# Norm sums by a row of ones and scales broadcast through DRAM, in a decoder layer of parallel mixers

## The chip, the cores and the metric

The kernel runs on one core of one Trainium2 chip. The metric is the device time of one execution in microseconds, as the median of several runs. A core has five engines with a queue each: TensorE (PE, matrix products; its weight loads are listed as PEld), VectorE (DVE), ScalarE (ACT), GpSimd (POOL) and SyncE (SP, which here issues most DMAs). Each engine takes its instructions in the order in which the program has them, and waits at an instruction until what it needs is there.

## The reference, cut to what matters

One layer on 1040 tokens (16 meta tokens and 1024 others) of 1024 channels. The places that the change touches are the sums of squares over channels, the pool map and their surroundings:

```python
h = rms_norm(h_res, pre_norm_g[i])
z = h @ w_in[i]                      # 1024 x 7328
(pv, pg, cq, ckv, kr, mg, cu, cg, sbcx, sg, gl) = split_cols(z)
# pool branch: four windows, then a 64 x 64 map per group
p = stack([(cs - lag) / cnt - g ...]); y = einsum('blgc,gcd->blgd', p, pool_w) * pool_scale
# latent attention
q  = rms_norm(c_q, q_norm_g) @ w_uq        # 256 channels, 8 heads of 64 + 32
kv = rms_norm(c_kv, kv_norm_g) @ w_ukv     # 128 channels
# conformer branch, after its depthwise convolution of width 31
z = silu(layer_norm(z, ln_g, ln_b))        # 256 channels
# short convolution of width 3, then gates, output projections, sum
m = sum(sigmoid(g_i) * y_i); x = x + rms_norm(m @ w_o, post_norm_g)
```

## The kernel before

**Three stages.** First the projection `z = h @ w_in`: channels on partitions, tokens on the free axis, 128 + 128 output channels times two halves of the tokens at a time, by seven half-size products instead of eight (a Strassen-like scheme). A product is split in three rounded passes: a number is held as a rounded high part and the rest (type float32r), and high x high, high x low and low x high are added up. The seven products of a pair of column blocks go to the PSUM banks `ps_pa`, `ps_pb`, `ps_pc` and `ps_pd`, 84 passes of 512 columns a pair, or two units of 84 passes of 256 or 272 columns where the meta tokens are among them. Then attention by heads (`ps_s` scores, `ps_o` outputs), with the output projections of three branches (`ps_y<-bo,whl`) put between. Then attention's own output projection and the last product with `w_o`.

**Side tasks.** Everything else of the first stage stands in four lanes of tasks (`task_conv`, `task_kv`, `task_q`, `task_norm`, `task_short`, `task_pool`, `task_w`, `task_so`, `task_first`). After each product of the projection `pump` advances each lane by its pace (0.9, 0.9, 1.1 and 0.5 steps). The list `pairs` sets the order of the column blocks; a task begins once the columns that it needs are written. The tasks' data lie in DRAM between steps (`z_dram` and others), and their tiles come from small rings of buffers (`t4`, `t2`, `w1`).

**What sets the order.** All instructions are first recorded, then a planner (`Plan.flush`) sorts them by a priority and by its own durations for engines and transfers, and issues each engine's instructions in that order. The engines then take them as they stand. Each instruction is issued at one line, so that views of the profile show L362 for nearly all, and one reads by tiles.

**Norm sums before** (`rs_row`, lines 943 to 969). The squares `sq` lie with channels on partitions. For 128 tokens at a time they are the stationary operand of a full-precision product with a column `ones`, so that a column of 128 sums comes out (`ps_x<-ones,sqk` and the like, four columns in a set). DVE divides and adds epsilon, POOL raises to the power -0.5 (`rs`). Four transposes of the columns, each widened to 128, put the scale of each token on all partitions (`ps_x<-ident,rs`), and DVE multiplies with it out of PSUM. `task_kv` does so for 512, 512 and 16 tokens, `task_q` twice, `task_norm` twice. `task_norm` also has a mean: a full-precision product of 512 columns with ones (`ps_y<-lsq,ones`). `task_pool` has four full-precision products of 512 columns with its map (`ps_y<-pd,pw`).

**Attention's start.** `load_q`, `load_kv` and the loads of masks, ones and zeros (lines 1438 to 1457) are issued on SP as the first stage's buffers come free. For head 0 the maxima of the scores are found in the first stage (`task_first`, once per half of the tokens) and come through `top_dram`.

Of the kernel before, what the change touches and what calls it, by code (L numbers as in the profile page):

```python
# [68 lines left out]
CH_KV = [(0, 512), (512, 512), (1024, 16)]  # L69
# [402 lines left out]
def trunk_kernel(ctx, tc, a):  # L472
# [34 lines left out]
    DVE.memset(ones, 1.0)  # L507
    mhalf = const.tile([P, 16], F32, name="mhalf")
# [29 lines left out]
    ones_dram = dram.tile([4, L], F32, name="ones4")  # L538
    top_dram = dram.tile([4, 2, 4, P], F32, name="top")
# [403 lines left out]
    def rs_row(sqs, of, scale=None, tag="x", ns=0):  # L943

        n = sqs[0].shape[1]
        p = min(n, P)
        if len(sqs) > 1:  # L950
            add(POOL, sqs[0], sqs[0], sqs[1])
        sq = sqs[0]
# [5 lines left out]
        rs = col([P, 4], "rs")[:p, :n // p]  # L958
        with plan.late(ns):
            DVE.tensor_scalar(rs, pc, 1.0 / of, EPS, op0=ALU.mult, op1=ALU.add)  # L960
            POOL.tensor_tensor(rs, rs, mhalf[:p, :n // p], op=ALU.pow)
        if scale:
            DVE.tensor_scalar(rs, rs, scale, None, op0=ALU.mult)
        yield
        out = bank(tag)[:, :n]
        for j in range(n // p):
            PE.transpose(out[:, p * j:p * (j + 1)], rs[:, j:j + 1].to_broadcast([p, P]), ident[:p, :p])
        yield
        return out
# [77 lines left out]
    def task_norm(c):  # L1047
# [5 lines left out]
        sq = [t2([P, 512], name="lsq")]  # L1053
        add(POOL, sq[0], acc[0], acc[1])
        pa = bank("y")
        PE.matmul(pa, ones.to_broadcast([P, P]), sq[0], start=True, stop=True)
        yield
        sq.append(t2([P, 512], name="lsq"))
# [4 lines left out]
        rs = yield from rs_row(sq, 256, tag="y")  # L1063
        for m in range(2):
            g, b, hb = (t_[:, r + m:r + m + 1] for t_, r in ((par, R_LG), (par, R_LB), (par, R_HLB)))
            DVE.scalar_tensor_tensor(acc[m], acc[m], g, rs, op0=ALU.mult, op1=ALU.mult)
            th, cg = t2([P, 512], name="lth"), t2([P, 512], name="cgt")
            ACT.activation(th, acc[m], AF.Tanh, scale=0.5, bias=hb)
            ld(cg, z_dram[f"cg{m}"][:, s_])
# [3 lines left out]
            mul(POOL, cg, acc[m], cg)  # L1073
            store_bo(2 + m, c, cg)
            yield

    def task_short(m, c):
# [5 lines left out]
        ld(xx, z_dram[f"x{m}"][:, p0:p0 + 514])  # L1083
        mul(POOL, u, u, xx)
        yield
        v = t2([P, 512], name="v")
# [7 lines left out]
        b, g = t2([P, 512], name="bt"), t2([P, 512], name="gt")  # L1094
        ld(b, z_dram[f"b{m}"][:, s_])
        ld(g, z_dram[f"sg{m}"][:, s_])
# [5 lines left out]

    def task_pool(m, c):

        s_ = slice(512 * c, 512 * (c + 1))
        pw = tp.tile([P, P], F32, tag="wraw", bufs=2, name="pw")
        POOL.memset(pw, 0.0)
        for g in range(2):
            ld(pw[64 * g:64 * g + 64, 64 * g:64 * g + 64], a["pool_w"][0, 2 * m + g])
        n = 512 + 15  # L1110
        pv_, sa, sb = (t2([P, n], name=i) for i in ("pv", "sa", "sb"))
        pd = t2([P, 512], name="pd")
        p0 = NM - 15 + 512 * c
        ld(pv_, z_dram[f"pv{m}"][:, p0:p0 + n])
        yield
# [10 lines left out]
        yield  # L1126
        pa = bank("y")
        g = t2([P, 512], name="pgt")
        ld(g, z_dram[f"pg{m}"][:, s_])
        PE.matmul(pa, pw, pd, start=True, stop=True)  # L1130
# [17 lines left out]
    def task_q(c):  # L1148
# [3 lines left out]
        cq, sq = t4([P, 2, 512], name="cq"), t4([P, 2, 512], name="sqq")  # L1152
        for m in range(2):
            ld(cq[:, m], z_dram[f"cq{m}"][:, s_])
            ACT.activation(sq[:, m], cq[:, m], AF.Square)
        yield
        rs = yield from rs_row([sq[:, 0], sq[:, 1]], 256, QK ** -0.5)
# [65 lines left out]
    def task_first(c):  # L1223

        n = NM + 512 * (c + 1)
        for h in range(FIRST):
            k_ = t4([QK, L], F32R, name="k0")[:, :n]
            k_rows(k_, h, lambda x: x[:, 0, :n])
            q_ = t4([QK, 512], F32R, name="q0")
            ld(q_, q_dram[c][h][:, 0])  # L1230
# [3 lines left out]
            mx = tp.tile([P, 4, 3], F32, name="mx")  # L1234
            POOL.memset(mx, NEG)
            yield from row_maxima(c, mx, q_, k_, mask, bank)
            mr = tp.tile([P, 4], F32, name="mr")
            DVE.tensor_reduce(mr, mx, axis=AX.X, op=ALU.max)
            pm = bank()
            PE.transpose(pm[:4, :P], mr, ident)  # L1240
            DVE.tensor_copy(mask[:4].bitcast(F32R), pm[:4, :P])
            for r in range(4):
                ld(top_dram[r:r + 1, c, r], mask[r:r + 1])

    def task_kv():
# [25 lines left out]
        ckv, sq = t4([P, L], name="ckv"), t4([P, L], name="sqk")  # L1271
        ld(ckv, z_dram["ckv"])
        ACT.activation(sq, ckv, AF.Square)
        yield
        for n0, n in CH_KV:
            rs = yield from rs_row([sq[:, n0:n0 + n]], P, ns=1500)
            DVE.scalar_tensor_tensor(ckv[:, n0:n0 + n], ckv[:, n0:n0 + n], par[:, R_KVG:R_KVG + 1], rs,
# [666 lines left out]
```

## Time and profile before

| | before |
|---|---|
| runs | 967.77, 968.78, 968.97 us, median 968.78 |
| span of the profiled execution, first to last instruction | 967.1 us (its time as a run is not given apart) |
| granted PE clock, mean | 0.998 |
| first scores of attention | 639.4 us |
| DMA | 203.03 MB, mean 210 GB/s |

How to read the lines that follow in the prediction. The busy table gives busy time, share of the span and count of instructions of each engine. A stretch row gives a stretch in us, its length, then busy us (and count) of PE, PEld, DVE, ACT and POOL, the granted clock, the DMA engines' busy share and GB/s. A row of the order of time gives start, length, engine, line, operation, out<-in, shape and a count; neighbours of one kind are merged, and what stands in brackets is the idle time before it and what ended it. A row of the groups ends with busy us and mean ns of one, then the idle time before. Matmuls overlap, so that a row's length runs into the next row's start.

### The profile page before, as it was taken

How to read it: one execution, taken by the hardware profiler on the slowest of the kernel's cores; microseconds unless marked ns; L12 is line 12 of the kernel's file. 1: busy time of each engine (PE TensorE's matmuls, PEld its weight loads, DVE VectorE, ACT ScalarE, POOL GpSimd, SP SyncE). 2: the span in 40 equal slices, each digit the busy share in tenths (PEclk: the TensorE clock that was granted, in tenths of full speed). 3: DMA queues.
4: the chain of work that ended last, by engine and by line, in shares of the span. 5: the costliest groups of instructions: out<-in, count | busy, mean ns of one | idle time of the engine just before them, and what ended most of it. 6: DMA issues, size and time to landing. Idle time of an engine off the chain costs nothing.

```text
span 967.1 us, 15246 instructions
## 1 busy us (share of the span) xinstructions
PE 952.0 (98%) x5003; PEld 809.9 (84%) x5003; DVE 692.5 (72%) x1111; ACT 449.4 (46%) x914; POOL 680.3 (70%) x630
## 2 busy tenths in 40 slices
PE   8999999999999999999999999999999999999996
PEld 7999899889888887888788878888888878788885
DVE  5856959988879855554446767436878888799857
ACT  7743233444443455554434344356555565324622
POOL 5957555666577887896679679656567786747955
PEclk9999999999999999999999999999999999999999
DMA  7144556758787687787655687699899663773543
GB/s 258 32 126 144 170 190 213 234 195 257 230 261 260 206 250 207 212 264 216 211 161 160 204 267 274 222 316 264 266 227 289 194 196 116 261 255 109 187 148 142
DMA packets 136329, 203.03 MB, mean 210 GB/s; under 512 B 19671, under 2 KB 83158, under 8 KB 135482
## 3 DMA queue, kind: packets, MB, share of 16 engines
q1 hardware_dynamic: 127274, 185.28, 62.2%
q10 hardware_dynamic: 8656, 15.74, 4.4%
q0 software_dynamic: 320, 1.05, 0.3%
q8 instruction: 39, 0.64, 0.3%
q14 instruction: 40, 0.33, 0.1%
HBM read 129.11 MB, written 72.88 MB: 209 GB/s over the span
## 4 chain that ended last, share of the span: by engine, by line
PE 88%; POOL 4%; DVE 3%; issue 2%; ACT 1%; DMA 1%; SPq 0%; DVEq 0%; ACTq 0%; POOLq 0%
PE ps_pa L362 16%; PE ps_pb L362 16%; PE ps_pc L362 15%; PE ps_o L362 9%; PE ps_u L362 7%; PE ps_s L362 7%; PE ps_pd L362 7%; PE ps_y L362 6%; PE ps_x L362 5%; POOL S L362 1%; DMA x<-in_x_dram 1%; POOL lsq L362 1%; DVE th L362 1%; POOL pt L362 0%; ACT junk L362 0%
## 5 line engine op out<-in xcount | busy, mean ns | idle before, releaser
L362 PE MATMUL ps_pb<-T,S 128*128 128x512 f32 (+2 forms) x792 | 172.0, 359 | 0.0
L362 PE MATMUL ps_pa<-B,A 128*128 128x512 f32 (+2 forms) x792 | 171.7, 360 | 0.0
L362 POOL TENSOR_TENSOR A<-raw,A 128x512 fp32r<-128x512 f32 x84 | 113.9, 1363 | 61.2 <-ACT A L362 51.5
L362 POOL TENSOR_TENSOR S<-ss,S 128x512 fp32r<-128x512 f32 x84 | 116.0, 1393 | 53.3 <-ACT S L362 53.2
L362 PEld LDWEIGHTS ps_pb<-T,S 128*128 128x128 f32 x792 | 134.3, 189 | 22.4 <-issue 1.2
L362 PEld LDWEIGHTS ps_pa<-B,A 128*128 128x128 f32 x792 | 134.4, 188 | 22.3 <-issue 1.0
L362 POOL TENSOR_TENSOR pt<-p,pt 128x512 fp32r<-128x512 f32 (+1 forms) x96 | 102.7, 1096 | 52.8 <-PE ps_s L362 31.4
L362 DVE TENSOR_TENSOR u<-ps_pb,u 128x512 f32<-128x512 f32 (+2 forms) x66 | 40.3, 611 | 87.2 <-PE ps_pb L362 84.1
L362 DVE SCALAR_TENSOR_TENSOR ps_w<-conv,par,ps_w 128x512 f32<-128x512 f32 x116 | 87.2, 752 | 2.3
L362 PE MATMUL ps_pc<-B,S 128*128 128x512 f32 (+1 forms) x396 | 85.9, 358 | 0.0
L362 ACT ACTIVATE S<-ss 128x512 fp32r<-128x512 f32 x84 | 50.5, 627 | 75.6 <-DVE ss L362 47.2
L362 PE MATMUL ps_y<-bo,whl 128*128 128x512 f32 x288 | 85.2, 404 | 0.3 <-DVE th L362 0.2
L362 PE MATMUL ps_pd<-T,A 128*128 128x512 f32 (+2 forms) x396 | 84.9, 359 | 0.0
L362 PE MATMUL ps_pc<-T,S 128*128 128x512 f32 (+1 forms) x396 | 84.4, 359 | 0.0
L362 ACT ACTIVATE p<-ps_s 128x512 f32<-128x512 f32 (+4 forms) x112 | 49.8, 444 | 58.0 <-PE ps_s L362 28.1
L362 PEld LDWEIGHTS ps_pc<-T,S 128*128 128x128 f32 x396 | 66.8, 188 | 11.2 <-issue 0.7
L362 PEld LDWEIGHTS ps_pd<-T,A 128*128 128x128 f32 x396 | 67.1, 189 | 10.7
L362 PEld LDWEIGHTS ps_pc<-B,S 128*128 128x128 f32 x396 | 66.4, 189 | 10.2
L362 PE MATMUL ps_o<-pt,vt 128*128 128x512 f32 (+7 forms) x288 | 69.1, 347 | 0.1
L362 PE MATMUL ps_s<-qt,kt 100*128 100x512 f32 (+4 forms) x336 | 68.9, 324 | 0.0
L362 PEld LDWEIGHTS ps_s<-qt,kt 100*128 100x128 f32 (+1 forms) x336 | 54.3, 176 | 10.6 <-DVE mxs L362 0.5
L362 ACT ACTIVATE A<-raw 128x512 fp32r<-128x512 f32 x84 | 52.0, 626 | 22.1 <-PE ps_pd L362 9.6
(282 smaller groups left out, 1891.6 us busy)
## 6 DMA issues: line engine op xcount, KB each, us to landing
raw<-in_w_in_dram SPq DMA_DIRECT2D x52, 512.0 KB
th<-th SPq DMA_DIRECT2D x32, 512.0 KB
th<-z ACTq DMA_DIRECT2D x60, 256.0 KB
v<-vhl SPq DMA_DIRECT2D x16, 384.0 KB
qt<-q SPq DMA_DIRECT2D x16, 384.0 KB
vt<-v SPq DMA_DIRECT2D x8, 768.0 KB
bo<-bo SPq DMA_DIRECT2D x6, 1024.0 KB
w_out_mla<-whl SPq DMA_DIRECT2D x16, 256.0 KB
```

The source lines that it names most:

```text
L362: getattr(self.handle[o["eng"]], o["op"])(*map(real, o["args"]), **{k: real(v) for k, v in o["kw"].items()})
```

## The change

1. `rs_row` is rewritten. The squares' sum is split in a rounded high and a low half (`sqh`, `sql`). A column of ones (`ones_r`, rounded) is the stationary operand, and both halves stream past it: 512 tokens give one row of 512 sums in two rounded passes. DVE evacuates the row to one partition (`row`). A DMA spreads the row over partitions (`rs`), POOL takes the power there, a DMA stores the scales to DRAM (`row_dram`), and the users load them from there to all partitions (`rsb`).
2. The norm's mean is two rounded passes (`lsh`, `lsl`) in place of a full-precision product. The pool map is split once per map (`pwhl`) and its products are three rounded passes. Several intermediate tiles (`v`, `pd`, sums, `th`) move from SBUF to PSUM banks.
3. The tasks are regrouped: `task_row_kv`, `task_row_q` and `task_kr` are apart from `task_kv` and `task_q`; `task_first` does both halves of the tokens at once; the sums for `w_o` (`task_so`) are cut into smaller tiles and spread over three lanes. The paces are 0.9, 1.05, 1.4 and 0.5. In `pairs` the columns of q, the pool and its gate come earlier.
4. Attention's first tiles lie in another order in SBUF, and the loads for head 0 (ones, keys, mask, values) stand ahead of those for head 1.

**The PE queue around kv's sums, before.** `sqk` are the squares of kv, `rs` the scales; `ps_pa` to `ps_pd` are the projection.

```order
L362 MATMUL ps_pc<-B_325,S_1348 128x512 x3
L362 MATMUL ps_x<-ones,sqk 128x1 x4
L362 MATMUL ps_pc<-B_325,S_1348 128x512 x9
L362 MATMUL ps_pa<-B_234,A_1412 128x256 x12
L362 MATMUL ps_pb<-T_564,S_1449 128x256 x12
L362 MATMUL ps_pc<-T_531,S_1456 128x256
L362 MATMUL ps_x<-ident,rs 128x128 x4
L362 MATMUL ps_x<-ones,sqk 128x1 x4
L362 MATMUL ps_pc<-T_531,S_1456 128x256 x11
```

**The PE queue around kv's sums, after**, one pair earlier in the program.

```order
L361 MATMUL ps_pc<-T_540,S_1018 128x512 x12
L361 MATMUL ps_x<-sqh,ones_r 1x512
L361 MATMUL ps_x<-sql,ones_r 1x512
L361 MATMUL ps_x<-sqh,ones_r 1x512
L361 MATMUL ps_x<-sql,ones_r 1x512
L361 MATMUL ps_pb<-T_323,S_1028 128x512 x4
L361 MATMUL ps_x<-sqh,ones_r 1x16
L361 MATMUL ps_x<-sql,ones_r 1x16
L361 MATMUL ps_pb<-T_323,S_1028 128x512 x8
```

The column products and the transposes are gone from PE; six passes stand together, and no scale comes back to PE.

**The PE queue around the norm of the first 512 tokens, before.** `lsq` is first the sum of the two channel blocks (for the mean), then the sum of their squares.

```order
L362 MATMUL ps_y<-lsq,ones 128x512
L362 MATMUL ps_pb<-T_564,S_4241 128x512 x6
L362 MATMUL ps_pc<-T_531,S_4247 128x512 x12
L362 MATMUL ps_pb<-T_316,S_4270 128x512 x12
L362 MATMUL ps_y<-ones,lsq 128x1 x4
L362 MATMUL ps_pd<-T_587,A_4301 128x512 x12
L362 MATMUL ps_pa<-B_257,A_4285 128x512 x5
L362 MATMUL ps_y<-ident,rs 128x128 x4
L362 MATMUL ps_pa<-B_257,A_4285 128x512 x6
```

**The same place after.** `lsh` and `lsl` are the halves of the sum, `sqh` and `sql` those of the squares.

```order
L361 MATMUL ps_y<-lsh,ones_r 128x512
L361 MATMUL ps_y<-lsl,ones_r 128x512
L361 MATMUL ps_pa<-B_239,A_4621 128x512 x7
L361 MATMUL ps_x<-cqn_4323,whl 128x512 x2
L361 MATMUL ps_pa<-B_239,A_4621 128x512 x2
L361 MATMUL ps_pb<-T_573,S_4677 128x512 x9
L361 MATMUL ps_x<-cqn_4323,whl 128x512
L361 MATMUL ps_x<-cqn_4328,whl 128x512 x3
L361 MATMUL ps_pb<-T_573,S_4677 128x512 x3
L361 MATMUL ps_pc<-T_540,S_4683 128x512
L361 MATMUL ps_y<-sqh,ones_r 1x512
L361 MATMUL ps_y<-sql,ones_r 1x512
```

Mean and squares take two passes each, and the transposes of `rs` are gone.

**SP's queue around the load of kv, before.** `raw` are the next pair's columns of w_in, `wraw` output weights of the branches.

```order
L362 DMA z_a_1228<-z 128x2x256
L362 DMA kr<-krh 128x260
L362 DMA ckv<-z_ckv 128x1040
L362 DMA w_out_pool_1408<-whl 128x512
L362 DMA kr<-krl 128x260
L362 DMA wraw<-in_w_out_pool_dram 128x2x128
L362 DMA z_cq_1465<-z 128x512 x2
L362 DMA raw<-in_w_in_dram 128x4x256
```

**After**, at the broadcast of kv's scales. `row` is the row of sums on one partition, here of q.

```order
L361 DMA pgt<-z_pg_1718 128x512
L361 DMA rsb<-row_kv 128x1040
L361 DMA ckv<-z_ckv 128x1040
L361 DMA rsx<-row 128x1x8
L361 DMA z_a_1879<-z 128x16
L361 DMA raw<-in_w_in_dram 128x4x256
L361 DMA z_a_1879<-z 128x2x256
L361 DMA raw<-in_w_in_dram 128x4x256
```

Two transfers of the new chains stand ahead of the next pair's `raw`, which had only its own stores and weights ahead of it.

The diff, cut to its core:

```diff
+    ones_r = const.tile([P, 1], F32R, name="ones_r")
+    copy(ones_r, ones)
+    row_dram = {k: dram.tile([n], F32, name=f"row_{k}")
+                for k, n in (("kv", L), ("q", NT), ("n0", 512), ("n1", 512))}
...
-    def rs_row(sqs, of, scale=None, tag="x", ns=0):
-        pc = bank(tag)[:p, :n // p]
-        for j in range(n // p):
-            PE.matmul(pc[:, j:j + 1].in_order(), sq[:, p * j:p * (j + 1)], ones, start=True, stop=True,
-                      skip_group_check=True)
...
-        for j in range(n // p):
-            PE.transpose(out[:, p * j:p * (j + 1)], rs[:, j:j + 1].to_broadcast([p, P]), ident[:p, :p])
+    def rs_row(sq, of, name, tile, tag="x", scale=None, beside=None):
+        hi, lo = halved(sq, tile, "sq", DVE if sq.buf.psum else POOL)
...
+        for n0 in range(0, n, 512):
+            m = min(512, n - n0)
+            pr = bank(tag)[:1, :m]
+            PE.matmul(pr, ones_r, hi[:, n0:n0 + m], start=True, stop=False)
+            PE.matmul(pr, ones_r, lo[:, n0:n0 + m], start=False, stop=True)
+            DVE.tensor_scalar(row[:, n0:n0 + m], pr, 1.0 / of, EPS, op0=ALU.mult, op1=ALU.add)
+        rs = tp.tile([P, 16], name="rs" + tag)[:n // cols, :cols]
+        ld(rs, row.rearrange("o (p c) -> o p c", c=cols))
+        yield
+        POOL.tensor_tensor(rs, rs, mhalf[:n // cols, :cols], op=ALU.pow)
+        if scale:
+            DVE.tensor_scalar(rs, rs, scale, None, op0=ALU.mult)
+        ld(row_dram[name].rearrange("(p c) -> p c", c=cols), rs)
...
-        PE.matmul(pa, ones.to_broadcast([P, P]), sq[0], start=True, stop=True)
+        for i in range(2):
+            PE.matmul(pa, ones_r.to_broadcast([P, P]), hl[i], start=i == 0, stop=i == 1)
...
-        PE.matmul(pa, pw, pd, start=True, stop=True)
+        PE.matmul(pa, whl[:, 0], ph, start=True, stop=False)
+        PE.matmul(pa, whl[:, 0], pl, start=False, stop=False)
+        PE.matmul(pa, whl[:, 1], ph, start=False, stop=True)
...
-        lane((("ckv", "kr"), task_kv), (("cq0", "cq1"), task_q, 0), ((), task_q, 1), ((), task_consts), ((), task_first, 0), ((), task_first, 1),
-             *[((), task_so, k) for k in range(KH)],
-             ): 0.9,
+        lane((("ckv", "kr"), task_row_kv), ((), task_kr), (("cq0", "cq1"), task_row_q), ((), task_kv), ((), task_q, 0), ((), task_q, 1), ((), task_consts), ((), task_first),
+             *[((), task_so, k, so_pairs, slice(0, 512)) for k in range(2)],
+             ): 1.05,
...
-    load_q(0, 0)
-    kt = [qk.tile([NA, 2, LK], F32R, name=f"kt{i}") for i in range(2)]
...
+    load_q(0, 0)
+    ld(kt[0][QK:NA, 0, :L], ones_dram)
+    k_rows(kt[0][:, :, :L], 0, lambda x: x)
+    ld(maskT, mask_dram[1])
+    ld(vt[0].rearrange("p j c -> p (j c)"), v_dram[0][0][:, 0:8].rearrange("p j c -> p (j c)"))
```

More of the change, by code (lines that the diff above doesn't have):

```diff
@@ L1052, in task_norm @@
             ld(acc[m], acc_dram[m][:, s_])
-        sq = [t2([P, 512], name="lsq")]
-        add(POOL, sq[0], acc[0], acc[1])
+        s = bank("y")
+        add(DVE, s, *acc)
+        yield
+        hl = halved(s, t2, "ls", DVE)
         pa = bank("y")
-        PE.matmul(pa, ones.to_broadcast([P, P]), sq[0], start=True, stop=True)
+        for i in range(2):
+            PE.matmul(pa, ones_r.to_broadcast([P, P]), hl[i], start=i == 0, stop=i == 1)
         yield
-        sq.append(t2([P, 512], name="lsq"))
+        sq = [t2([P, 512], name="lsq") for m in range(2)]
         for m in range(2):
@@ L1072, in task_norm @@
             yield
-            mul(POOL, cg, acc[m], cg)
-            store_bo(2 + m, c, cg)
+            mul(POOL, cg[m], acc[m], cg[m])
+            store_bo(2 + m, c, cg[m])
             yield
@@ L1270, in task_kv @@
         yield
[L1271 removed]
+    def task_kv():
+        rs, ckv = t4([P, L], name="rsb"), t4([P, L], name="ckv")
+        ld(rs, row_dram["kv"].partition_broadcast(P))
         ld(ckv, z_dram["ckv"])
[L1273 removed]
         yield
[L1275 to L1278 removed]
+        DVE.scalar_tensor_tensor(ckv, ckv, par[:, R_KVG:R_KVG + 1], rs, op0=ALU.mult, op1=ALU.mult)
         yield
```

180 lines of the change are left out of this document (112 added, 68 removed).

## The prediction

> **What bounds the kernel now.** I read the busy table first, then the chain of work that ended last, then the busy time by stretches, and last the order of time on PE.
>
> ```profile
> PE 952.0 (98%) x5003; PEld 809.9 (84%) x5003; DVE 692.5 (72%) x1111; ACT 449.4 (46%) x914; POOL 680.3 (70%) x630
> PE 88%; POOL 4%; DVE 3%; issue 2%; ACT 1%; DMA 1%; SPq 0%; DVEq 0%; ACTq 0%; POOLq 0%
> 150.00:200.00 50.00, 50.00 (x261) 43.33 (x260) 45.09 (x67) 20.53 (x43) 35.03 (x30) 1.00 0.67 210
> 300.00:640.00 340.00, 339.22 (x1506) 277.53 (x1505) 198.04 (x260) 152.46 (x277) 262.56 (x235) 1.00 0.72 222
> ```
>
> PE is busy for 98% of the span and carries 88% of the chain. In the stretch rows the second number is PE: 50.00 of 50, and 339.22 of 340 up to the start of attention. The granted clock is 1.00 in both. The next engine is DVE, 45.09 of 50 in the tightest stretch. So in the projection, which lasts until about 639 us, **time is PE's instruction stream**: what leaves that stream leaves the kernel, until DVE or a wait takes its place. Ends of matmuls are modelled, so I take every price from starts:
>
> ```profile
> 587.71 2.88 PE L362 MATMUL ps_pc<-T,S 128*128 128x512 f32 x12
> 590.43 2.88 PE L362 MATMUL ps_pb<-T,S 128*128 128x512 f32 x12
> ```
>
> Twelve rounded passes of 512 columns take 590.43 - 587.71 = 2.72 us, 0.227 us each. That is the unit for all that follows: a piece of side work costs the distance between the starts around it, less 0.227 for each ordinary pass in between.
>
> **What leaves PE: column sums.** A sum over partitions was four full-precision products that give one column each (two records per product).
>
> ```profile
> 108.17 0.84 PE L362 MATMUL ps_pc<-B,S 128*128 128x512 f32 x3
> 108.85 0.95 PE L362 MATMUL ps_x<-ones,sqk 128*128 128x1 f32 x8
> 109.66 2.34 PE L362 MATMUL ps_pc<-B,S 128*128 128x512 f32 x9
> 111.84 1.59 PE L362 MATMUL ps_pa<-B,A 128*128 128x256 f32 x12
> ...
> 572.11 1.52 PE L362 MATMUL ps_pd<-T,A 128*128 128x512 f32 x6
> 573.48 0.95 PE L362 MATMUL ps_y<-ones,lsq 128*128 128x1 f32 x8
> 574.28 1.65 PE L362 MATMUL ps_pd<-T,A 128*128 128x512 f32 x6
> 575.77 2.45 PE L362 MATMUL ps_pa<-B,A 128*128 128x512 f32 x10
> 578.55 0.65 PE L362 MATMUL ps_y<-ident,rs 128*128 128x128 f32 x4 [0.34 <-POOL rs L362]
> 578.96 0.71 PE L362 MATMUL ps_pa<-B,A 128*128 128x512 f32 x2
> 579.51 2.92 PE L362 MATMUL ps_pc<-B,S 128*128 128x512 f32 x12
> ```
>
> The first of six sets costs 111.84 - 108.17 - 2.72 = 0.95 us, the last 575.77 - 572.11 - 2.72 = 0.94. Six sets (two each of kv, q and norm): 6 x 0.94 = **5.6 us**.
>
> **What leaves PE: broadcasts.** The scales came back across partitions by four transposes each. The last set above costs 579.51 - 575.77 - 2.72 = 1.02, with a wait of 0.34 for POOL's power in it. The cheapest lies together with a column set:
>
> ```profile
> 114.70 0.28 PE L362 MATMUL ps_pc<-T,S 128*128 128x256 f32 x1
> 114.82 0.60 PE L362 MATMUL ps_x<-ident,rs 128*128 128x128 f32 x4
> 115.25 0.95 PE L362 MATMUL ps_x<-ones,sqk 128*128 128x1 f32 x8
> 116.06 1.55 PE L362 MATMUL ps_pc<-T,S 128*128 128x256 f32 x11
> 117.45 1.60 PE L362 MATMUL ps_pb<-T,S 128*128 128x256 f32 x12
> 118.89 1.60 PE L362 MATMUL ps_pd<-T,A 128*128 128x256 f32 x12
> ```
>
> Twelve passes of 256 columns take 118.89 - 117.45 = 1.44, so the two sets here cost 117.45 - 114.70 - 1.44 = 1.31, and the transposes 1.31 - 0.95 = 0.36. Between 0.36 and 1.02 I take the middle, 0.69, times six: **4.1 us** (2.2 to 6.1 if all were like one end). The last sixteen tokens of kv had one short product and one narrow transpose of their own: a quarter of 0.94 and of 0.36, **0.3 us**.
>
> **What leaves PE: full-precision products of 512 columns.** Two for the norm's mean and four for the pool map.
>
> ```profile
> 371.08 1.02 PE L362 MATMUL ps_y<-lsq,ones 128*128 128x512 f32 x2
> 371.54 1.95 PE L362 MATMUL ps_pb<-T,S 128*128 128x512 f32 x6
> 373.33 2.90 PE L362 MATMUL ps_pc<-T,S 128*128 128x512 f32 x12
> ...
> 457.28 2.66 PE L362 MATMUL ps_pb<-T,S 128*128 128x512 f32 x11
> 459.77 1.02 PE L362 MATMUL ps_y<-pd,pw 128*128 128x512 f32 x2
> 460.23 0.80 PE L362 MATMUL ps_pb<-T,S 128*128 128x512 f32 x1
> 460.87 2.92 PE L362 MATMUL ps_pc<-T,S 128*128 128x512 f32 x12
> ```
>
> The mean costs 373.33 - 371.08 - 6 x 0.227 = 0.89; the map 460.87 - 457.28 - 2.72 = 0.87. Six of them: 2 x 0.89 + 4 x 0.87 = **5.3 us**. Gone in all: 5.6 + 4.1 + 0.3 + 5.3 = 15.3 us.
>
> **What comes to PE.** Rounded passes of 512 columns: 8 for the kv and q rows, 4 for the norm rows, 4 for the means, 12 for the pool map (three each), 28 in all, and two of 16 columns. The row products have only one output partition. Whether that changes their pace is bounded by these two groups:
>
> ```profile
> L362 PE MATMUL ps_x<-wvhl,ckh 128*128 128x256 f32 x32 | 6.5, 283 | 0.0
> L362 PE MATMUL ps_x<-wvhl,ckh 128*16 128x256 f32 x4 | 0.8, 279 | 0.0
> ```
>
> With 16 stationary columns a pass takes 279 ns where one with 128 takes 283, so I cost a row pass as any other: 28 x 0.227 = 6.4 us, and 0.1 at most for the two short ones. **Net on PE: 15.3 - 6.5 = 8.8 us.** The merged first-head maxima save one narrow transpose; I cost that at nothing.
>
> **What is hidden, and by what.** The squares, splits, sums and row evacuations go to ACT, POOL and DVE, under PE's passes. For DVE that is twelve steps of 512 columns on PSUM (sums and low halves) and seven rows of one partition. The nearest is an evacuation of 512 columns:
>
> ```profile
> L362 DVE TENSOR_TENSOR u<-ps_pb,u 128x512 f32<-128x512 f32 x46 | 31.7, 689 | 70.7 <-PE ps_pb L362 69.6 <-issue 0.9
> ```
>
> At 689 ns each, 19 steps are 13 us at most over 590 us, less the small steps that go. Where DVE already has 45.09 of 50, the worst case is that PE gives back the excess: 4 us. The regrouping only moves the remaining tasks (pool earlier, w_o sums into other lanes); it changes none of PE's counts. It costs nothing while DVE, POOL and the queue keep ahead, and up to those 4 us otherwise.
>
> The scale now makes **three transfers in a row** (row to columns, columns to DRAM, broadcast back), all on SP's queue. The nearest such trip is attention's own:
>
> ```profile
> 668.92 0.33 SPq L362 DMA_DIRECT2D r<-lc  x1
> 678.98 0.47 SPq L362 DMA_DIRECT2D rb<-r  x1
> ...
> 600.72 3.52 SPq L362 DMA_DIRECT2D raw<-in_w_in_dram  x2
> ...
> 620.35 2.88 PE L362 MATMUL ps_pa<-B,A 128*128 128x512 f32 x12
> ```
>
> From one issue to the next 10.06 us pass there, part of it by the plan. Three such steps are 30 us per chain at the most. I take nothing, since in the new order some 84 us of other passes stand on PE between kv's last row pass and the first product that needs the scaled kv, and some 216 us for q; behind the norm's scale PE has nothing. If that cover were gone, PE would wait the 30 us. What stands behind a held transfer on SP is the next pair's w_in (the order above): it is issued at 600.72, both halves by 604.24, and first used at 620.35, 16 us later.
>
> The Trainium skill, "DMA: Bandwidth & Descriptors", section "Anatomy of one DMA — SWDGE (gpsimd) path", gives about 2.0 us fixed for each DMA however small, and so speaks against replacing on-chip transposes by three small transfers. By it a chain would be an estimated 6 us of latency. No row here times an SP transfer's landing alone; the 10.06 us above is not less than the page says. As the chain ends no PE wait, the sum stays the same by page and by row.
>
> **Attention's first loads.** Before, they cost PE nothing:
>
> ```profile
> 613.37 0.46 SPq L362 DMA_DIRECT2D qt<-q  x1
> ...
> 639.39 3.16 PE L362 MATMUL ps_s<-qt,kt 100*128 100x512 f32 x18
> ```
>
> Loads start at 613.37; the first scores follow the last projection pass (636.67 + 2.72 = 639.39) with no gap. So their new order can gain nothing, and the cover is the last pair's passes, 26 us. The maxima of head 0 now come later: in the new order their transpose has 171 passes of 512 columns before the first scores (3 of the pair's product and 14 whole products), 39 us for two small steps and a load.
>
> **Sum.** The span is 967.1 us; the runs' median, 968.78, is 1.7 above it, and I keep that offset. 968.78 - 8.8 = **960.0 us**.
>
> **Rivals.** (a) *DVE becomes the bound* where it has 45 of 50, or PE meets new short waits for the halves that ACT and DVE now cut: for it, DVE's row above and the six waits of the old broadcasts; against it, PE's 50.00 in that very stretch. It gives back up to 4 us: 964. (b) *SP's queue holds w_in back*, slower than before: four chains, each with a transfer that waits for the one before. If each holds the queue for 10 us and half of the 16 us of lead is used up by landing and the split, 2 to 4 us of PE stall per chain are left, 8 to 16 in all, so 968 to 976; from 2.7 us a chain (10.8 in all) it is slower than before. Against it: DMA share 0.67 to 0.72 in the projection. (c) *One-column rounded passes run at full-precision price*, 0.87 each: 12 x 0.64 = 8 us back, 968, no change. The 16-column row speaks against it. (d) *More is gained*: broadcasts near the upper end (6.1 instead of 4.1) and fewer stray waits later: 957.
>
> **How the numbers follow.** Forecast 960.0, by itself 958 to 962.5, chance 0.66. (a) 0.16, (d) 0.08, (b) 0.06, (c) and the like 0.04. The range 956.5 to 965.5 takes in the forecast, (d) and (a). A measurement of this kernel can tell about 0.2%, 1.9 us, from no change. Faster: forecast, (a), (d), 0.90; same: (c) and the mild end of (b), 0.06; slower: 0.04.
>
> **What would show it.** In the profile after: no record of one-column products or scale transposes; row passes 0.227 us apart; PE still at 98%; first scores near 630.6 instead of 639.4, and the same distance from there to the end. Wrong if PE shows waits before the row or pool passes, if DVE has over 48 of 50, or if w_in is late.

## The result, and the profile after

The changed kernel takes 960.64 us (median of 4 runs, 959.63 to 962.45) beside 968.29 us for the kernel before (4 runs, 967.77 to 968.97). The ratio is 0.9922, with a 95% interval of 0.991 to 0.9934: 0.8% faster. The profiled execution was the fastest of the four, 959.63 us, with a span of 957.9.

The busy table and the chain of the page of the changed kernel:

```profile
PE 943.9 (99%) x4945; PEld 804.2 (84%) x4945; DVE 720.2 (75%) x1124; ACT 453.5 (47%) x925; POOL 677.7 (71%) x627
PE 92%; DVE 3%; POOL 2%; issue 1%; ACT 1%; DMA 1%; SPq 0%; DVEq 0%; POOLq 0%; ACTq 0%
```

PE is the bound as before, with a larger share of the span and of the chain. Its busy time is 8.1 us less, in 58 records fewer. DVE has taken 27.7 us more (692.5 to 720.2). Where that is tightest shows in the busy time by stretches:

```profile
250.00:300.00 50.00, 50.00 (x232) 41.38 (x231) 49.10 (x65) 23.91 (x48) 37.94 (x35) 1.00 0.72 229
300.00:630.00 330.00, 330.00 (x1463) 272.01 (x1463) 215.03 (x289) 149.44 (x279) 238.03 (x225) 1.00 0.78 239
```

DVE, the third of the busy numbers, is at 49.10 of 50 from 250 to 300 us, and PE still has its 50.00. So the two run all but full beside each other there, and PE's row shows no wait.

The new passes on PE, in the order of time (kv's rows, the first norm's row):

```profile
78.03 0.40 PE L361 MATMUL ps_x<-sqh,ones_r 128*1 128x512 f32 x1
78.26 0.39 PE L361 MATMUL ps_x<-sql,ones_r 128*1 128x512 f32 x1
78.49 0.39 PE L361 MATMUL ps_x<-sqh,ones_r 128*1 128x512 f32 x1
78.72 0.39 PE L361 MATMUL ps_x<-sql,ones_r 128*1 128x512 f32 x1
78.95 1.09 PE L361 MATMUL ps_pb<-T,S 128*128 128x512 f32 x4
...
409.87 0.40 PE L361 MATMUL ps_y<-sqh,ones_r 128*1 128x512 f32 x1
410.11 0.40 PE L361 MATMUL ps_y<-sql,ones_r 128*1 128x512 f32 x1
410.35 0.86 PE L361 MATMUL ps_pc<-T,S 128*128 128x512 f32 x3
```

Four row passes take 78.95 - 78.03 = 0.92 us, 0.23 each: a stationary operand of one column costs what one of 128 costs. No row waits.

Four starts divide the span: the first product of the second kind (`ps_pc<-T,S`), the first scores, the first product of attention's output (`ps_u<-boM`), and the end. Of the kernel before and of the changed one:

```profile
55.25 1.60 PE L362 MATMUL ps_pc<-T,S 128*128 128x256 f32 x12
...
838.38 3.79 PE L362 MATMUL ps_u<-boM,whl 128*128 128x512 f32 x16
```

```profile
53.65 1.60 PE L361 MATMUL ps_pc<-T,S 128*128 128x256 f32 x12
...
629.38 0.86 PE L361 MATMUL ps_s<-qt,kt 100*128 100x512 f32 x3
...
829.38 12.86 PE L361 MATMUL ps_u<-boM,whl 128*128 128x512 f32 x56
```

| part, us | before | after | difference |
|---|---|---|---|
| start, to the first `ps_pc<-T,S` | 55.25 | 53.65 | -1.6 |
| projection, to the first scores | 584.14 | 575.73 | -8.4 |
| attention, to the first `ps_u<-boM` | 198.99 | 199.99 | +1.0 |
| rest | 128.69 | 128.48 | -0.2 |
| span | 967.07 | 957.86 | -9.2 |

So the gain is where the forecast had it, in the projection, and two smaller terms that it did not have stand beside it.

The projection's rows can also be counted by the prediction's own rule, over the whole stretch: the distance from start to start, less the usual 0.227, 0.125 or 0.120 us of an ordinary pass of 512, 272 or 256 columns. What an ordinary pass takes beyond that is put down to the side work up to six passes ahead of it (or, with none there, up to three behind it).

| side work on PE, us | before, counted | predicted to leave | after, counted | predicted to come |
|---|---|---|---|---|
| column sums; then row passes | 5.7 | 5.8 | 3.0 | 2.8 |
| broadcasts by transposes | 4.7 | 4.2 | 0 | 0 |
| means | 1.8 | 1.8 | 0.9 | 0.9 |
| pool map | 3.6 | 3.5 | 2.8 | 2.7 |
| sum of the unrounded terms | 15.7 | 15.3 | 6.7 | 6.5 |

By this count the net that leaves PE is 9.0 us, where 8.8 were predicted. That the stretch is shorter by 8.4 and not by 9.0 is spread over all other rows in amounts too small to assign.

### The profile page after: what moved, and what is told of

Its sections match the earlier page's. It is cut to its first block, busy times and chain, and to the rows that moved or that the text cites. A ratio compares the mean times of both kernels' runs of the same rounds, so it can differ in the third digit from the quotient of the medians.

```text
span 957.9 us, 15219 instructions
## 1 busy us (share of the span) xinstructions
PE 943.9 (99%) x4945; PEld 804.2 (84%) x4945; DVE 720.2 (75%) x1124; ACT 453.5 (47%) x925; POOL 677.7 (71%) x627
## 3 DMA queue, kind: packets, MB, share of 16 engines
q0 software_dynamic: 320, 1.05, 0.3%
## 4 chain that ended last, share of the span: by engine, by line
PE 92%; DVE 3%; POOL 2%; issue 1%; ACT 1%; DMA 1%; SPq 0%; DVEq 0%; POOLq 0%; ACTq 0%
PE ps_pa L361 17%; PE ps_pb L361 17%; PE ps_pc L361 16%; PE ps_o L361 9%; PE ps_pd L361 8%; PE ps_u L361 7%; PE ps_s L361 7%; PE ps_y L361 6%; PE ps_x L361 4%; DMA x<-in_x_dram 1%; DVE th L361 1%; POOL pt L361 0%; ACT junk L361 0%; DVE op L361 0%; DVE c L361 0%
## 5 line engine op out<-in xcount | busy, mean ns | idle before, releaser
L361 PEld LDWEIGHTS ps_pa<-B,A 128*128 128x128 f32 x792 | 134.2, 188 | 21.2 <-issue 0.2
L361 PE MATMUL ps_pc<-B,S 128*128 128x512 f32 (+1 forms) x396 | 83.7, 357 | 0.0
L361 DVE TENSOR_TENSOR z<-ps_pc,u 128x512 f32<-128x512 f32 (+1 forms) x64 | 38.8, 606 | 33.9 <-PE ps_pc L361 27.4
```

The costliest lines, as they stand in the source:

```text
L361: getattr(self.handle[o["eng"]], o["op"])(*map(real, o["args"]), **{k: real(v) for k, v in o["kw"].items()})
```

## The experiments

The kernel before was run beside each group on the same chip: median 968.55 us for the first four kernels, 969.26 for the next four, 968.33 for the last four. "Proj." and "att." are the second and third part of the table above, from each run's profile.

| run | time, us | ratio to before, 95% | start | proj. | att. |
|---|---|---|---|---|---|
| changed kernel again | 960.03 | 0.9908 [0.9894, 0.9921] | 53.94 | 575.71 | 200.05 |
| ones rounded on DVE | 960.62 | 0.9913 [0.9900, 0.9927] | 54.83 | 575.80 | 200.03 |
| before, with an early step on ACT | 968.97 | 1.0001 [0.9991, 1.0012] | 55.75 | 584.49 | 199.25 |
| columns and transposes back | 969.84 | 1.0007 [0.9995, 1.0018] | 54.52 | 584.63 | 200.31 |
| columns, scales still through DRAM | 988.68 | 1.0180 [1.0148, 1.0212] | 54.11 | 601.69 | 203.05 |
| full-precision products back | 969.64 | 1.0003 [0.9981, 1.0025] | 54.28 | 582.29 | 200.01 |
| second trip through DRAM, all rows | 988.40 | 1.0185 [1.0157, 1.0213] | 54.43 | 598.66 | 206.60 |
| old order of tasks | 977.80 | 1.0075 [1.0054, 1.0095] | 54.09 | 583.68 | 210.22 |
| second trip, norms' rows alone | 978.54 | 1.0115 [1.0093, 1.0137] | 54.22 | 588.84 | 209.87 |
| second trip, kv's and q's rows alone | 964.17 | 0.9957 [0.9941, 0.9974] | 54.46 | 578.64 | 200.27 |
| changed, attention's old loads | 960.77 | 0.9924 [0.9909, 0.9938] | 54.02 | 575.73 | 199.83 |
| before, attention's new loads | 969.47 | 1.0011 [1.0001, 1.0022] | 54.09 | 584.04 | 200.23 |

### The start

The changed kernel once more, without an edit:

> The changed kernel again, as the yardstick of this chip. Compared by stretches: up to the first ps_pc pass of the projection (before 55.2 us, after 53.7), from there to attention's first scores (584.1 before, 575.7 after), from there to the first ps_u pass (199.0 before, 200.0 after), and the rest (129). If the early start is the chance of one execution, the first stretch lies anywhere between 53.7 and 55.2; if it comes from the program, at 53.7 again. Ratio to before 0.991 to 0.993.

It came out at 960.03, with the parts of the first profile within 0.3 us. The order of ACT's first steps differs between the two kernels: the rounding of `ones` makes ACT load its table at 1.36 us instead of 4.34. Two runs take this away and bring it alone, one in the changed kernel and one in the kernel before:

```diff
-    copy(ones_r, ones)
+    DVE.tensor_copy(ones_r, ones)
```

> Only the rounded column of ones is made by DVE and not by ACT, so that ACT's first activation is again the one that waits for x. Theory A: ACT's table load (1.28 us) stands ahead of its first activation and waits with it; the copy of the ones brought it forward under the load of x. Then the first stretch goes back from 53.7 to about 55.2 (+1.3 to +1.6) and the whole is 1.3 to 1.6 us over the changed kernel. Theory B: the early start is from the transfers of x, which landed earlier by chance or by their order; then the first stretch stays at 53.7.

```diff
+    ones_r = const.tile([P, 1], F32R, name="ones_r")
+    copy(ones_r, ones)
```

> The kernel before, with one more ACT copy of a 128 x 1 column of ones at the very start, which nothing reads. Theory A (table load brought forward): first stretch 53.7 in place of 55.2, the whole 1.3 to 1.6 us faster than before (ratio about 0.9985). Theory B: nothing, 1.000.

The early table load alone gave the kernel before nothing: ratio 1.0001, start 55.75. Without it the changed kernel took 960.62, 0.6 us more than in the repeat and not the 1.3 to 1.6 of theory A; the start of its profile was 54.83. The order of time on ACT in the kernel before with the early step shows why:

```profile
1.36 1.28 ACT L362 ACT_TABLE_LOAD   x1 [1.36 <-PEq L1935]
4.89 1.06 ACT L362 ACTIVATE junk<-x 128x1024 bf16<-128x1024 f32 x1 [2.02 <-DMA x<-in_x_dram]
8.14 1.06 ACT L362 ACTIVATE junk<-x 128x1024 bf16<-128x1024 f32 x1 [2.10 <-DMA x<-in_x_dram]
```

The table is there at 1.36, and ACT then waits for the second tile of the input until 8.14. In the profile of the changed kernel that tile's squares start at 6.83, in the kernel before at 8.52. Over all profiles the start lies between 53.65 and 54.83 us for the changed kernel and its variants, and between 54.09 and 55.75 for the three of the kernel before and its variants. The two overlap, and the start moves with the landing of the input's tiles. So the 1.6 us of the first comparison cannot be counted as a gain of the change; that a smaller part of it is lasting, up to about 1 us, these few profiles do not exclude.

### The parts of the projection's gain

Column sums and transposes back, on the changed kernel's grouping, so that the columns never leave the core:

```diff
-            PE.matmul(pr, ones_r, hi[:, n0:n0 + m], start=True, stop=False)
-            PE.matmul(pr, ones_r, lo[:, n0:n0 + m], start=False, stop=True)
...
+            PE.matmul(pc[:p, j:j + 1].in_order(), sq[:, P * j:P * j + p], ones, start=True, stop=True,
+                      skip_group_check=True)
...
+            PE.transpose(out[:, P * j:P * j + p], col_of[name][:p, j0 + j:j0 + j + 1].to_broadcast([p, P]), ident[:p, :p])
```

> The changed kernel with norm sums by full-precision column products and scales spread by PE transposes, as before; all else (tasks, lanes, pool map, means, attention's loads) as changed. Theory A (PE's stream alone): the column sets (5.6) and transposes (4.4) come back, 12 row passes (2.8) go: projection stretch +7.2 us, from 575.7 to about 583, the whole about 968 (ratio 0.999). Rival (it was the regrouping of tasks that brought the time): stretch within 2 us of 575.7.

The projection took 584.63 us, 8.9 more than the changed kernel, and the time was that of before (1.0007). The waits of PE in its projection:

```profile
PE ps_pb L361 <- DVE u L361: 1.0, 1, 1.0
PE ps_y L361 <- DVE pdl L361: 0.7, 1, 0.7
```

The changed kernel has 0.2 of the first and none of the second. So some 1.5 of the 8.9 us are named waits. Counted by the rule above, sums (5.6) and broadcasts (3.2) come back and the row passes (3.0) go, 5.8 us in all, where 7.2 were expected. The remaining 1.6 us are short hold-ups of PE that the waits do not name. The new order of the tasks with the old sums in it is worth nothing: this kernel still has the cheaper means and pool map, and is no faster than before.

The six full-precision products of 512 columns back, the rest as changed:

```diff
-        for i in range(2):
-            PE.matmul(pa, ones_r.to_broadcast([P, P]), hl[i], start=i == 0, stop=i == 1)
+        PE.matmul(pa, ones.to_broadcast([P, P]), s, start=True, stop=True)
...
-        PE.matmul(pa, whl[:, 0], ph, start=True, stop=False)
-        PE.matmul(pa, whl[:, 0], pl, start=False, stop=False)
-        PE.matmul(pa, whl[:, 1], ph, start=False, stop=True)
+        PE.matmul(pa, whl, sa[:, :512], start=True, stop=True)
```

> The changed kernel with the norm's means and the pool map as full-precision products again (the pool's operand copied from PSUM to SBUF by ACT). Theory A: 2 x 0.89 + 4 x 0.87 = 5.3 us come, 16 rounded passes, 3.6, go: projection stretch +1.6, from 575.7 to 577.3. Rival (splits by ACT and DVE cost what the passes save): 575.7 or less.

This missed: the projection took 6.6 us more, and the runs scattered from 966.87 to 975.28, with a median of 969.64. The profile is of the fastest. Its waits, one stretch, and what DVE and ACT wait for in it:

```profile
PE ps_x L361 <- ACT cqn L361: 2.5, 1, 2.5
PE ps_x L361 <- DVE khl L361: 0.4, 1, 0.4
```

```profile
470.00:475.00 5.00, 2.48 (x11) 1.71 (x10) 1.52 (x3) 1.80 (x4) 2.80 (x3) 1.00 0.66 219
```

```profile
472.45 0.69 DVE L361 TENSOR_TENSOR z<-ps_pc,u 128x512 f32<-128x512 f32 x1 [2.28 <-DMA th<-z]
472.80 0.63 ACT L361 ACTIVATE A<-raw 128x512 fp32r<-128x512 f32 x1 [4.06 <-DMA th<-z]
```

From 470 to 475 PE has only 2.48 of 5 us, and DVE and ACT have less. The rows in the order of time show DVE and ACT waiting for a store of `z` to land, and PE stands at a product of q whose operand `cqn` comes behind them. That wait is not in the product that was changed. Together the named waits are 2.9 us. The products' own price, expected at 1.6, is 1.7 by the rule above (means 0.8, pool map 0.9). About 2 us of the 6.6 are not assigned.

The two undone parts add up to 8.9 + 6.6 = 15.5 us of projection, and the change as a whole gained 8.4. By the count of starts their own prices are 5.8 and 1.7, and the rest are waits and hold-ups that neither whole kernel has.

### How well the trip through DRAM is covered

Columns as before, but the scales still through DRAM. A column layout makes the store write single numbers of 4 bytes:

```diff
...
+        ld(row_dram[name][:m].rearrange("(c p) -> p c", p=P), rs[:, :n // P])
...
```

> The changed kernel with the sums by full-precision column products again (the columns stand on partitions at once, so the row's transfer over partitions falls away), but the scales still broadcast through DRAM. Theory A (PE's stream alone): six column sets and the short one, 5.6 + 0.2, come back and 12 row passes, 2.8, go: projection stretch +3.0, from 575.7 to 578.7; the further step to the run with transposes, 584.6, is then the transposes' 4 to 6 us with their waits. Rival (the transposes' removal brought all of it): 575.7 within 1 us.

It took 988.68 us. The largest wait of PE, and the stretches around it:

```profile
PE ps_pa L361 <- ACT z L361: 11.4, 1, 11.4
```

```profile
410.00:415.00 5.00, 5.00 (x23) 4.13 (x22) 3.21 (x6) 1.20 (x2) 0.57 (x1) 1.00 0.83 237
...
420.00:425.00 5.00, 0.00 (x0) 0.00 (x0) 0.00 (x0) 0.02 (x1) 0.75 (x1) 0.74 0.44 12
```

SP's rows there, of the store of the first norm's scales and of the load behind it:

```profile
414.86 1.82 SPq L361 DMA_DIRECT2D row_n<-rsy  x1
...
428.04 0.33 SPq L361 DMA_DIRECT2D rsb<-row_n  x1
```

The store is issued by 416.68 and carries 2 KB. From 420 to 425 PE, PEld, DVE and ACT do next to nothing, and the DMA engines are busy for 0.44 of the time, but move 12 GB/s, after 237 at 410 to 415 (last column). Behind each of the run's other three stores of scales (kv's, q's and the second norm's) there is such a stretch too:

```profile
90.00:95.00 5.00, 5.00 (x38) 4.73 (x38) 4.37 (x6) 1.02 (x2) 3.51 (x4) 1.00 0.41 4
...
140.00:145.00 5.00, 5.00 (x40) 5.00 (x41) 3.29 (x6) 1.25 (x4) 5.00 (x5) 1.00 1.22 16
...
495.00:500.00 5.00, 5.00 (x24) 4.08 (x22) 1.70 (x3) 3.00 (x8) 3.97 (x6) 1.00 1.05 25
```

The DMA engines are busy for 0.41 of the time and more (the view's share can exceed 1), and move 4 to 25 GB/s. There PE had work that needed no transfer. So 512 or 1024 numbers written one by one hold up nearly all other transfers, here for some 10 us, and then everything that needs one. The Trainium skill, "DMA: Bandwidth & Descriptors", says under "Rules for kernel authors" that a last dimension that is not contiguous becomes one descriptor per element, and under "Specifications" that below 512 bytes the DMA reads, modifies and writes; the trace agrees in kind, with 12 GB/s. In the changed kernel the row is spread so that each partition writes neighbouring numbers (four of them in the norms' rows), and no stretch of its projection shows busy DMA engines that move so little.

This run therefore says little of the column products, and more of how a store is laid out. For the trip itself, the scales were sent through DRAM a second time:

```diff
+        trip = dram.tile([n], F32, name=f"trip_{name}")
+        ld(trip.rearrange("(p c) -> p c", c=cols), rs)
+        back = tp.tile([P, 16], name="rs" + tag)[:n // cols, :cols]
+        ld(back, trip.rearrange("(p c) -> p c", c=cols))
-        ld(row_dram[name].rearrange("(p c) -> p c", c=cols), rs)
+        ld(row_dram[name].rearrange("(p c) -> p c", c=cols), back)
```

> The changed kernel with the trip through DRAM made twice: the scales go to DRAM, come back to the columns, and go to DRAM again, two more transfers in each of the four chains (kv, q, two norms). Theory A (84 us of passes and more cover the chain): projection stretch 575.7 as before, within 0.5. Rival (the chain, or SP held by it, already costs PE something): 1 us or more is added.

It took 988.40 us, and the projection 598.66, 22.9 more: theory A missed. The tasks in the order of before (short convolution, first norm, pool, second norm), with the new sums; the list `pairs` has its columns in the order that goes with it:

```diff
...
-        lane(*[((f"pv{m}", f"pg{m}"), task_pool, m, c) for m, c in halves]
-             + [((f"b{m}", f"c{m}", f"x{m}", f"sg{m}"), task_short, m, c) for m, c in halves]
-             + [((f"conv0{c}", f"conv1{c}", "cg0", "cg1"), task_norm, c) for c in range(2)]
+        lane(*[((f"b{m}", f"c{m}", f"x{m}", f"sg{m}"), task_short, m, c) for m, c in halves]
+             + [(("conv00", "conv10", "cg0", "cg1"), task_norm, 0)]
+             + [((f"pv{m}", f"pg{m}"), task_pool, m, c) for m, c in halves]
+             + [(("conv01", "conv11"), task_norm, 1)]
...
```

> The changed kernel with the columns of z and the third lane in the order of before (short convolutions, first norm, pool, second norm); paces and everything else as changed. Theory A (counts on PE decide): projection stretch 575.7 within 0.7. Rival (the order keeps DVE from falling behind; it has 49.1 of 50 us at 250 to 300 us in the changed kernel): PE gets waits, 2 to 4 us more.

It took 977.80 us; the projection took 8.0 us more, and the 0.7 of theory A and the 2 to 4 of its rival were both missed. Both runs have their longest wait at one place. The row of attention's first load on SP, and the first scores on PE, of the changed kernel, of the old order, and of the double trip:

```profile
607.95 1.10 SPq L361 DMA_DIRECT2D qt<-q  x1
```

```profile
622.50 0.38 SPq L361 DMA_DIRECT2D qt<-q  x1
...
637.76 1.49 PE L361 MATMUL ps_s<-qt,kt 100*128 100x512 f32 x3 [4.87 <-DMA qt<-q]
```

```profile
637.92 0.42 SPq L361 DMA_DIRECT2D qt<-q  x1
...
653.09 1.19 PE L361 MATMUL ps_s<-qt,kt 100*128 100x512 f32 x2 [21.23 <-DMA vs<-v]
```

In the last two the scores come 15.3 and 15.2 us after the load is issued. In the changed kernel the load is issued 21.4 us before the scores (629.38), so that about 6 us are to spare. The loads stand on SP's queue behind the stores of the sums for `w_o` (`so<-so`), whose third part is the last task of the norms' lane. If this is the cause, the second trip of the norms' rows alone must bring the wait, and that of kv and q must not. Both edits are in effect the one above, with `if name in ("n0", "n1")` or `if name in ("kv", "q")` around it:

> The changed kernel with the scales sent a second time through DRAM, for the two layer norms' rows alone (in the double trip of all four, TensorE waited 21.2 us before the first scores; attention's first load was issued at 637.9 instead of 608.0 us). Theory T, the tail of the norms' lane: the second norm and the third part of the w_o combinations behind it end late, attention's first loads queue behind their stores on SP, and the first scores come 15 us after the first load. Then this run has most of it: first load at 630 to 640, a wait of 14 to 24 us before the first scores, projections about 590 to 600 us, span about 972 to 985. Theory C, what counts is the longer trip of kv's and q's rows (later k, q and v, later stores): the first load comes before 614, no wait over 1 us there, span about 958 to 960.

> The changed kernel with the second trip through DRAM for the rows of kv and q alone. Theory T: the lane of k, q and v has the cover, attention's first load is issued before 614 us, the waits of TensorE in the projections stay under 2 us and the span at 958 to 961. Theory C: the first load is issued at 630 to 640, a wait of 14 to 24 us stands before the first scores, and the span is 972 to 985. Rival to both, each trip takes a part of one common cover: the first load is issued between, near 620, with 4 to 6 us of wait, and the other run shows a wait as long.

The norms' rows alone took 978.54 us (977.96 to 983.47). The profile is of the slowest of the four:

```profile
620.36 7.80 SPq L361 DMA_DIRECT2D so<-so  x4
628.25 0.38 SPq L361 DMA_DIRECT2D qt<-q  x1
...
643.06 1.19 PE L361 MATMUL ps_s<-qt,kt 100*128 100x512 f32 x2 [10.51 <-DMA kt<-kr]
```

The first load follows the stores `so<-so` at once. It is 20 us late, and the scores follow 14.8 us behind it. The wait is 10.5 us, less than the 14 to 24 expected; the first load is late by less than in the run with all four. The rows of kv and q alone took 964.17 us with the first load at 603.49, earlier than in the changed kernel. PE has no named wait before the first scores. The cost is in short waits of the projection:

```profile
PE ps_x L361 <- ACT cqn L361: 0.9, 1, 0.9
PE ps_y L361 <- DVE pdl L361: 0.5, 1, 0.5
PE ps_x L361 <- DVE vhl L361: 0.5, 1, 0.5
PE ps_pb L361 <- DVE u L361: 0.2, 1, 0.2
```

So the tail of the norms' lane is shown as the place where a longer trip costs. The expectation for kv and q was missed by a little (waits under 2 us expected and 2.1 named, span 962.4 instead of 958 to 961). Neither run alone explains the 28 us of all four rows (18 and 4); how they combine was not followed further.

### Attention's loads

The old order of tiles and loads in the changed kernel, and the new order in the kernel before (the diff is part 4 of the change, backwards and forwards):

> The changed kernel, with attention's tiles and first loads written in the order of before. Theory A, the 1.0 us that attention loses (199.0 us before, 200.0 after, from the first scores to the first products with w_o) comes from that order: the two waits of TensorE that only the changed kernel has (0.74 us for p near 632.4, 0.67 us for ol near 711) go, attention takes 199.0, the projections stay at 575.7, and the time falls by 1.0 us, to about 959.2. Theory B, the order of the loads is not what makes them: attention stays at 200.0 and the time at 960.2 or, if the first scores now wait for a later load, above that.

> The kernel of before, with attention's tiles and first loads in the new order alone. Theory A (the new order makes the two waits): attention goes from 199.0 to 200.0 us with waits near 641.8 and 720.5, and the time rises by 1.0 us, to about 969.5. Theory B: attention stays at 199.0 and the time within 0.5 us of before.

In the kernel before, the new order brings both waits, as theory A has it. First the order of time of before at that place, then with the new loads:

```profile
642.38 0.40 PE L362 MATMUL ps_o<-pt,vt 128*128 128x512 f32 x1
642.63 0.96 PE L362 MATMUL ps_s<-qt,kt 100*128 100x512 f32 x3
643.49 0.33 PE L362 MATMUL ps_s<-kt,qt 96*128 96x144 f32 x1
```

```profile
641.12 0.39 PE L362 MATMUL ps_o<-pt,vt 128*128 128x512 f32 x1
641.37 0.33 PE L362 MATMUL ps_s<-kt,qt 96*128 96x144 f32 x1
642.22 0.50 PE L362 MATMUL ps_s<-qt,kt 100*128 100x512 f32 x1 [0.52 <-ACT p L362]
...
721.19 1.19 PE L362 MATMUL ps_o<-pt,vt 128*128 128x512 f32 x4 [0.52 <-ACT ol L362]
```

With the loads in another order the planner puts the narrow scores (144 columns) ahead of three wide ones, and PE then waits 0.52 us for ACT's step on `p`. The last row is the second wait. From the first `kt,qt` scores on, the whole order of PE in attention is the same in this kernel and in the changed one, and differs from that of before. Attention takes 200.23 us, 1.2 more, and the time is 1.0011 of before, interval 1.0001 to 1.0022.

The reverse gave nothing: with the old loads the changed kernel has PE's old order in attention and neither of the two waits, but attention takes 199.83 us and the time is 960.77. Other short waits come instead (the longest is 0.4 us, for DVE's masked scores near 651); they are only a part of the difference. Why the same order on PE runs 0.8 us slower here than in the kernel before stays open.

## Why the prediction was right

**The bound and the net on PE.** PE's stream was the time, and 8.8 us were to leave it; the projection lost 8.4. The split into terms holds as well, not only the net: counted over all rows of both profiles, 15.7 us left (15.3 predicted) and 6.7 came (6.5). Sums and broadcasts carry most of it. The broadcasts are the least exact term, 4.7 us where 4.2 were taken, from the middle of a range; the prediction's price (up to 1.02 us a set) contained waits, and so does the count. The runs with a part undone cost more than their terms, because new waits come with them.

**The price of new passes.** 0.227 us was taken for each, also with one stationary column; they take 0.23 (and 0.24 for the norm's two). Rival (c) is out.

**DVE.** Rival (a) is out for this kernel, though closer than it looked: DVE rose to 49.10 of 50 at 250 to 300, above the 48 that the prediction called a sign against it, and PE kept its 50.00. That sign was set too low: a second engine that is all but full was no loss here, as PE's row shows no wait. The price of DVE's work was wrong, though: 13 us at most were counted, and 27.7 came. The nineteen new steps take 14.1, about as counted. But steps that were taken as unchanged got longer. Those that multiply by the scales now read them from SBUF instead of PSUM, here the norm's, before and after:

```profile
L362 DVE SCALAR_TENSOR_TENSOR lacc<-lacc,par,ps_y 128x512 f32<-128x512 f32 x4 | 2.8, 744 | 3.4 <-PE ps_y L362 3.4
```

```profile
L361 DVE SCALAR_TENSOR_TENSOR lacc<-lacc,par,rsb 128x512 f32<-128x512 f32 x4 | 6.3, 1604 | 0.0
```

One takes 1604 ns instead of 744. And 56 sums of columns of `w_in` (`ss<-raw` and `ss<-raw,ss`), which the change does not touch, take 73.5 us instead of 60.7; no run shows why. The prediction had not allowed for this; it does not show in the time, since PE had no wait for it.

**The cover of the trip.** "I take nothing" was right for this kernel: PE's only named wait between 54 and 630 us is 0.2 us long. The cover that was counted is there: from kv's last row pass to the first product of scaled kv 84.4 us pass (79.90 to 164.30), and for q 216.6 (145.79 to 362.39). The chain itself is longer than the "30 us per chain at the most": from the first norm's row pass at 409.87 to the first step that reads its broadcast scales, at 446.55, it is 36.7 us. And the step that says that behind the norm's scale PE has nothing was wrong. Behind it stand the rest of the lane, its stores on SP's queue, and attention's first loads. The spare time there was about 6 us, and a longer trip passed it at once. The prediction had not looked at it, so that this term came out at nothing is in part luck. Rival (b) put the danger at `w_in`; the old order and the two double trips that include the norms show the queue's delay at attention's loads, with 4.9, 10.5 and 21.2 us of wait.

**The regrouping** was costed at nothing, as moving work alone. With the old sums in it, it gains nothing (the run with columns and transposes), but the new sums need a good order: with the tasks of that one lane, and the column blocks that feed it, in the order of before, attention's first load comes late and the kernel takes 977.80 us, slower than before. That price was missing from the prediction.

**Attention's first loads.** "Can gain nothing" was right, but it was priced at 0 with the same distance from there to the end, and attention takes 1.0 us more. In the kernel before, the new order of the loads alone brings 1.2 us and the same two waits. The step failed because it counted only when loads land; the order of the loads also changes the order that the planner gives to all of attention. Taking the order back did not take the loss back, so that a part of it stays open.

**The start** had no term. Its 1.6 us in the profiled pair go with the landing of the input's tiles, and the starts of the two kernels' variants overlap. In the spans the parts are -8.4, +1.0, -1.6 and -0.2, together -9.2. The medians differ by 7.7: the profiled execution of the changed kernel is its fastest, 1.0 us under its median, and that of the kernel before, with the span 1.7 us below the time as in the changed kernel, is an estimated 0.5 us above its own. In the repeat the difference was 8.5.

No kernel that was run beats the changed one.

## What to carry to other kernels

When one engine is full, price a change by what leaves and enters that engine's stream, from distances between starts, and not by the length of rows. A latency that is moved off the chip is free only as far as its lane's last consumer has time to spare: follow the lane to its end, the stores that it leaves on a shared queue and the first loads of the next stage included, and state the spare time as a number. Where a planner orders the work, undoing one part does not give that part's price, because new waits come with the new order.

## What was not expected of the hardware

A store of 2 KB in single numbers of 4 bytes stopped nearly all traffic: 12 GB/s for 5 us with the DMA engines 0.44 busy, and an 11.4 us wait of PE (the run with columns and scales through DRAM). The other three stores of that run show the same, with 4 to 25 GB/s.

A wait also lowers PE's granted clock, and the clock comes back late. The stretches of the run with the second trip for the norms' rows alone:

```profile
635.00:640.00 5.00, 0.00 (x0) 0.00 (x0) 0.00 (x0) 0.00 (x0) 0.15 (x4) 0.59 1.03 268
...
643.00:653.00 10.00, 9.84 (x34) 8.28 (x34) 1.25 (x5) 5.20 (x13) 4.07 (x6) 0.50 0.99 246
653.00:656.00 3.00, 3.00 (x15) 2.46 (x15) 0.61 (x2) 2.73 (x5) 1.82 (x2) 1.00 1.02 418
...
675.00:680.00 5.00, 5.00 (x15) 4.03 (x15) 2.38 (x7) 1.42 (x3) 1.27 (x1) 0.50 1.00 283
```

The granted clock, third number from the end, falls in the wait (0.59 is the mean of that stretch). PE works at 0.50 from 643 to 653 us, and at 1.00 from there. So the wait of 10.5 us before the scores lengthens attention behind it as well, which took 9.9 us more than in the changed kernel; a later wait of 2.6 us, with PE at 0.50 behind it again (675 to 680), is also in that sum. The Trainium skill, "TensorE: Matmul & The Clock Gate", "What's actually happening", has half clock after an idle window of about 3.4 us and full clock after as long a busy one. The trace agrees with the half clock behind the long wait. It differs in two places, and the measurement decides: the full clock came back only about 10 us after PE had work again, with PE busy for 9.84 of them, and a wait of 2.6 us was enough for the half clock.
